# Moving GpSimd's elementwise work of a two-block network to VectorE and ScalarE

## The chip, the cores and the metric

The kernel runs on one core of a Trainium2 chip. The metric is the device time of one execution in microseconds (us). The engines are called as in the profile: PE (TensorE, the matmuls; PEld loads their weights), DVE (VectorE), ACT (ScalarE), POOL (GpSimd) and SP (SyncE, which issues DMAs).

## The reference

Everything is computed in fp32, for 256 tokens of width 1024. A first block has two layers (an mLSTM and a differential attention, each followed by a mixture of experts). A second block then runs two layers over two streams, the latent tokens `h` and 256 context tokens `hc`; each layer is a feed-forward, a mixer and a second feed-forward. Cut to what matters here:

```python
def pre(t, mm, i, gi):
    return rms_norm(t, g[gi]) * (1 + mm[:, :, i + 1]) + mm[:, :, i]
def post(t, y, mm, i, gi, wres):
    return t + wres * mm[:, :, i + 2] * rms_norm(y, g[gi])

h = post(h, swiglu(pre(h, m, 0, 0), ffn_wi[0], ffn_wo[0]), m, 0, 1, 0.5)     # hc alike
u, uc = pre(h, m, 3, 2), pre(hc, mc, 3, 2)
oc, kv_c = context_mix(uc @ w_in, qk_g, conv_w)      # last layer: only kv_c
o = latent_mix(u @ w_in, kv_c, cos, sin, qk_g, rpb, conv_w, rows)
h = post(h, o @ w_o, m, 3, 3, 1.0)                   # hc alike, but not in the last layer
h = post(h, swiglu(pre(h, m, 6, 4), ffn_wi[1], ffn_wo[1]), m, 6, 5, 0.5)
```

The mixers hold softmax attentions of 64-wide heads: six heads over latent and context keys (512), six with a position bias over a window of the latent keys and all context keys, and in the first layer twelve more of the context over its own 256 keys.

## The kernel before

Activations lie transposed: `xT` and `ctxT` hold the two streams as 8 slices of 128 features by 256 tokens. Each fp32 operand of a matmul is split into a high part that PE takes in one pass and the low rest, and a product is three matmuls (`mm3`, L381 to L383). Weights arrive by DMA as `raw` pieces; `chunks` makes the high part on ACT (L371) and the low part on DVE (L374). This goes on through the whole program.

The second block (`second_block`, from 1200 us on) runs six sublayers: feed-forward, mixer, feed-forward, twice. The first four carry both streams out, the last two only the latent one. Between two sublayers lies a transition, five in all. While a sublayer's output `y` comes out of PE, slice by slice and stream by stream, `Output.add` squares it (L497, L498 on ACT), takes its product with the old `x` (L499 on DVE), and adds these three 256-wide tiles into `acc` (L501, a 128x768 addition): on DVE for the last but one slice, else on POOL. After the last slice `sums` adds over the partitions with matmuls (L519), `rows` reads the sums (`rowsums`, L537), and `rstd` (L412 to L422) makes the reciprocal roots of `y` and of the new `x` with eleven tiny DVE instructions each; PE spreads a result over the partitions (L427). Then `update` goes slice by slice: `xs` is the scaled output (L561), `xT` takes it (L562, POOL but for the first slice), the new input is scaled (L569) and `split_sum` adds a shift and splits it into the parts `u` for the next matmuls: even slices with one ACT and one DVE instruction (L361, L362), odd ones with two on ACT and a subtraction on POOL (L357 to L359). `x_squares` (L461) does similar sums at the start of each block.

A mixer (`mix`) projects queries, keys and values, loads a position bias and turns its sign by 12 POOL subtractions (L904), and calls `attend` over units of two heads: six units of 512 keys in each of the two mixers, and six of 256 in the first. For a unit, `parts` splits keys and queries (high on ACT L838, low on POOL L839), PE makes scores, `softmax` takes the extreme on DVE (L818), exponentials with their sum on ACT (L822), the reciprocal on DVE (L824) and multiplies the row by it on POOL (L825). PE then transposes the weights (L860), an engine that the scheduler picks copies them out of PSUM (L861, ACT or DVE), and PE takes the values. While a unit's scores are made, the one before is transposed and multiplied; there are four buffers for `p`, two for `ysq`.

The order of every engine's instructions is not written by hand. A scheduler arranges the program from the written order, the dependences and its own estimate of each instruction, and chooses the engine of the free copies; so an instruction that moves to another engine shifts its neighbours too.

Of the kernel before, what the change touches and what calls it, by code (L numbers as in the profile page):

```python
# [13 lines left out]
AF = mybir.ActivationFunctionType  # L14
# [5 lines left out]
KT = 8  # L20
# [214 lines left out]
class Kernel:  # L235
# [114 lines left out]
        self.nc.scalar.activation(hi, src, AF.Copy)  # L350
        self.nc.vector.tensor_sub(lo, src, hi)  # L351

    def split_sum(self, hi, lo, src, col, by_pool=False):

        nc = self.nc
        if by_pool:
            nc.scalar.activation(src, src, AF.Identity, bias=col)  # L357
            nc.scalar.activation(hi, src, AF.Copy)
            nc.gpsimd.tensor_sub(lo, src, hi)  # L359
        else:  # L360
            nc.scalar.activation(hi, src, AF.Identity, bias=col)  # L361
            nc.vector.scalar_tensor_tensor(lo, src, col, hi, op0=ALU.add, op1=ALU.subtract)  # L362

    def chunks(self, ring, src, step=128):

# [86 lines left out]
    def x_squares(self, pool, s):  # L452

        nc = self.nc
        st = self.st()
        sums = []
        for k in range(KT):
            sq = pool.tile([128, S], F32, name="sq", **(dict(tag="sq", bufs=2) if k % 2 else dict(tag="xs", bufs=self.xs_bufs)))
            nc.scalar.activation(sq, self.xs(k, s), AF.Square)
            if k % 2:  # L460
                (nc.gpsimd if k < 4 else nc.vector).tensor_add(sums[-1], sums[-1], sq)  # L461
            else:
                sums.append(sq)
        for k, sq in enumerate(sums):
            for j in range(2):
                nc.tensor.matmul(st[:, j:j + 1], sq[:, j * 128:j * 128 + 128], self.ones[:, :1], start=(k == 0 and j == 0),
                                 stop=True, skip_group_check=True)
        return st[:, :2]
# [9 lines left out]
    class Output:  # L478
# [10 lines left out]
        def add(self, d, s):  # L489

            kern, nc = self.kern, self.kern.nc
            y = self.y(d, s)
            if d == 0:
                t = self.acc[s] = self.pool.tile([128, 3, S], F32, tag=f"acc{s}", name="acc", bufs=1)
            else:
                t = self.pool.tile([128, 3, S], F32, tag="pt", name="ysq", bufs=2)
            nc.scalar.activation(t[:, 0], y, AF.Square)  # L497
            nc.scalar.activation(t[:, 1], y, AF.Square, scale=self.gate(d, s))  # L498
            nc.vector.scalar_tensor_tensor(t[:, 2], y, self.gate(d, s), kern.xs(d, s), op0=ALU.mult, op1=ALU.mult)  # L499
            if 0 < d < KT - 1:  # L500
                (nc.vector if d == KT - 2 else nc.gpsimd).tensor_add(self.acc[s], self.acc[s], t)  # L501
            self.late.append(lambda: self.end(d, s, t))

        def go_on(self):
# [48 lines left out]
    def update(self, pool, u, s, out, gs, sh):  # L553

        nc = self.nc
        rb1, rb2 = out.rows(s)

        def add(k):
            if k < KT:
                t = pool.tile([128, S], F32, tag="xs", name="xs", bufs=self.xs_bufs)  # L560
                nc.vector.scalar_tensor_tensor(t, out.y(k, s), out.gate(k, s), rb1, op0=ALU.mult, op1=ALU.mult)  # L561
                (nc.gpsimd if k else nc.vector).tensor_add(self.xs(k, s), self.xs(k, s), t)  # L562

        for k in range(AHEAD):
            add(k)
        for k in range(KT):
            add(k + AHEAD)
            t = pool.tile([128, S], F32, tag="xs", name="xs", bufs=self.xs_bufs)
            nc.vector.scalar_tensor_tensor(t, self.xs(k, s), gs[:, k:k + 1], rb2, op0=ALU.mult, op1=ALU.mult)  # L569
            self.split_sum(u[:, k, 0], u[:, k, 1], t, sh[:, k:k + 1], k % 2)  # L570

    def scale_cols(self, pool, sc, g, ns, name):

# [240 lines left out]
    def softmax(self, pool, sc, n, scale=None):  # L814

        nc = self.nc
        mx = pool.tile([128, 4], F32, tag="mx", name="mx", bufs=8)
        nc.vector.tensor_reduce(mx[:, 0:1], sc[:, :n], axis=AX.X, op=ALU.min)  # L818
        if scale:
            nc.vector.tensor_mul(mx[:, 0:1], mx[:, 0:1], scale[0])  # L820
        p = pool.tile([128, 2 * S], F32, tag="p", name="p", bufs=4)
        nc.scalar.activation(p[:, :n], sc[:, :n], AF.Exp, bias=mx[:, 0:1], scale=scale[1] if scale else -1.0,  # L822
                             accum_out=mx[:, 1:2])
        nc.vector.reciprocal(mx[:, 2:3], mx[:, 1:2])  # L824
        nc.gpsimd.tensor_mul(p[:, :n], p[:, :n], mx[:, 2:3].to_broadcast([128, n]))  # L825
        return p

    def attend(self, ring, pool, units):
# [5 lines left out]
        def parts(q, k, nk, *_):  # L834

            out = ring.parts()
            for x, c in ((k[:, :nk], slice(0, nk)), (q, slice(512, 512 + S))):
                nc.scalar.activation(out[0][:, c], x, AF.Copy)  # L838
                nc.gpsimd.tensor_sub(out[1][:, c], x, out[0][:, c])  # L839
            return out  # L840

        def scores(qk, t, q, k, nk, v, vcols, out, bias, rs):
# [46 lines left out]
    def mix(self, ring, pool, l, u, out, u_home, proj_home):  # L889
# [11 lines left out]
        for t in range(2):  # L901
            nc.sync.dma_start(bias[:, t], A["rpb"][l, t])
            for h in range(6):
                nc.gpsimd.tensor_sub(bias[:, t, h], self.k("window_up"), bias[:, t, h])  # L904
        nc.vector.tensor_scalar(gq, self.v(f"qk_{l}_0"), -0.125, None, op0=ALU.mult)
        nq = TQ // 128
        offs = (0, 8, 8 + 2 * nq, 8 + 4 * nq)
# [957 lines left out]
```

## Time and profile before

| | us |
|---|---|
| runs | 2702.36, 2703.2, 2704.69 (median 2703.2) |
| the profiled execution | 2702.24 |
| its span | 2700.4 |
| busy: PE / PEld | 2476.7 (92%) / 1915.4 (71%) |
| busy: DVE / ACT / POOL | 1653.1 (61%) / 935.7 (35%) / 473.4 (18%) |

The span runs from the first to the last instruction of the profile. Busy shares are averages over stages with different limits; a row of idle time names what ended it.

### The profile page before, as it was taken

How to read it: one execution, taken by the hardware profiler on the slowest of the kernel's cores; microseconds unless marked ns; L12 is line 12 of the kernel's file. 1: busy time of each engine (PE TensorE's matmuls, PEld its weight loads, DVE VectorE, ACT ScalarE, POOL GpSimd, SP SyncE). 2: the span in 40 equal slices, each digit the busy share in tenths (PEclk: the TensorE clock that was granted, in tenths of full speed). 3: DMA queues.
4: the chain of work that ended last, by engine and by line, in shares of the span. 5: the costliest groups of instructions: out<-in, count | busy, mean ns of one | idle time of the engine just before them, and what ended most of it. 6: DMA issues, size and time to landing. Idle time of an engine off the chain costs nothing.

```text
span 2700.4 us, 38571 instructions
## 1 busy us (share of the span) xinstructions
PE 2476.7 (92%) x14614; PEld 1915.4 (71%) x14614; DVE 1653.1 (61%) x3421; ACT 935.7 (35%) x1641; POOL 473.4 (18%) x420
## 2 busy tenths in 40 slices
PE   3988997887999899999899999999899999898998
PEld 3874344566444688888775788888788888786997
DVE  7873125786222368656866777673858665958555
ACT  3541103564011232223327542222432223445543
POOL 2330101544000000002406420000400001534100
PEclk9989998888999899999899999999999999999999
DMA  8789997667999356532340236453247443322453
GB/s 320 276 327 410 420 419 261 232 211 298 381 398 419 141 185 221 168 120 88 135 138 1 79 110 209 154 190 91 74 148 226 155 150 97 118 83 94 160 178 123
DMA packets 123305, 540.62 MB, mean 200 GB/s; under 512 B 14688, under 2 KB 14944, under 8 KB 98272
## 3 DMA queue, kind: packets, MB, share of 16 engines
q1 hardware_dynamic: 123104, 538.00, 55.2%
q8 instruction: 119, 1.95, 0.3%
q14 instruction: 82, 0.67, 0.1%
HBM read 536.90 MB, written 1.05 MB: 199 GB/s over the span
## 4 chain that ended last, share of the span: by engine, by line
PE 56%; DVE 7%; issue 1%; ACT 1%; DMA 1%; POOL 0%; DVEq 0%; SPq 0%; ACTq 0%; POOLq 0%
PE mm L382 16%; PE mm L383 16%; PE mm L381 16%; DVE lo L374 2%; PE tp L383 1%; PE tp L382 1%; PE tp L381 1%; PE mm L868 1%; PE tp L860 1%; PE mm L848 1%; DVE ysq L499 1%; DMA raw<-in_w_ada_dram 1%; ACT hi L371 0%; DVE mx L818 0%; DVE rs_x L412 0%
## 5 line engine op out<-in xcount | busy, mean ns | idle before, releaser
L374 DVE TENSOR_TENSOR lo<-raw,hi 128x512 fp32r<-128x512 f32 (+1 forms) x780 | 574.7, 766 | 381.5 <-ACT hi L371 379.1
L371 ACT ACTIVATE hi<-raw 128x1024 fp32r<-128x1024 f32 (+1 forms) x390 | 404.7, 1044 | 872.3 <-PE mm L382 571.4
L381 PE MATMUL mm<-u,hi 128*128 128x512 f32 (+1 forms) x1608 | 572.8, 360 | 17.5 <-ACT hi L371 9.6
L383 PE MATMUL mm<-u,lo 128*128 128x512 f32 (+1 forms) x1608 | 576.8, 360 | 5.2 <-DVE lo L374 5.2
L382 PE MATMUL mm<-u,hi 128*128 128x512 f32 (+1 forms) x1608 | 578.2, 360 | 2.3 <-POOL u L359 1.3
L381 PEld LDWEIGHTS mm<-u,hi 128*128 128x128 f32 x1608 | 306.9, 193 | 64.5 <-ACT hi L371 11.2
L383 PEld LDWEIGHTS mm<-u,lo 128*128 128x128 f32 x1608 | 310.5, 193 | 49.1 <-DVE lo L374 6.9
L382 PEld LDWEIGHTS mm<-u,hi 128*128 128x128 f32 x1608 | 310.6, 193 | 47.3 <-DVE u L362 2.5
L382 PE MATMUL mm<-act,hi 128*128 128x512 f32 (+1 forms) x612 | 223.0, 364 | 0.1
L381 PE MATMUL mm<-act,hi 128*128 128x512 f32 (+1 forms) x612 | 222.3, 363 | 0.0
L383 PE MATMUL mm<-act,lo 128*128 128x512 f32 (+1 forms) x612 | 222.2, 363 | 0.0
L1691 PE MATMUL mm<-raw,xg 128*32 128x512 f32 x1696 | 199.2, 593 | 1.1 <-DMA raw<-in_moe_gu_dram 1.1
L623 DVE SCALAR_TENSOR_TENSOR junk<-raw,conds 128x1024 f32<-128x1024 f32 x128 | 155.6, 1222 | 66.3 <-DMA raw<-in_w_ada_dram 65.9
L620 POOL TENSOR_TENSOR raw<-raw,cond 128x1024 f32<-128x1024 f32 x48 | 119.9, 2502 | 244.7 <-DMA raw<-in_w_ada_dram 224.8
L501 POOL TENSOR_TENSOR acc<-acc,ysq 128x768 f32<-128x768 f32 x45 | 92.5, 2065 | 394.0 <-DVE ysq L499 348.8
L623 DVE SCALAR_TENSOR_TENSOR raw<-raw,conds 128x1024 f32<-128x1024 f32 x128 | 156.6, 1229 | 2.4
L628 POOL TENSOR_TENSOR mod<-mod,vecs 128x16 f32<-128x16 f32 (+1 forms) x28 | 10.3, 366 | 764.7 <-DVE raw L623 721.4
L1691 PEld LDWEIGHTS mm<-raw,xg 128*32 128x32 f32 x1696 | 63.0, 110 | 112.3 <-issue 107.6
L381 PEld LDWEIGHTS mm<-act,hi 128*128 128x128 f32 x612 | 117.5, 192 | 18.7 <-issue 1.2
L382 PEld LDWEIGHTS mm<-act,hi 128*128 128x128 f32 x612 | 117.7, 192 | 18.2 <-DVE act L351 0.7
L383 PEld LDWEIGHTS mm<-act,lo 128*128 128x128 f32 x612 | 117.5, 192 | 17.2
L1723 DVE TENSOR_TENSOR hy<-hy,tp 128x512 f32<-128x512 f32 x56 | 38.2, 686 | 149.3 <-PE tp L1720 149.1
(458 smaller groups left out, 4102.5 us busy)
## 6 DMA issues: line engine op xcount, KB each, us to landing
raw<-in_moe_gu_dram SPq DMA_DIRECT2D x122, 1024.0 KB, 17.8
raw<-in_w_ada_dram SPq DMA_DIRECT2D x200, 512.0 KB, 4.5
raw<-in_ffn_wi_dram SPq DMA_DIRECT2D x176, 512.0 KB, 4.3
raw<-in_moe_down_dram SPq DMA_DIRECT2D x63, 1024.0 KB, 17.8
raw<-in_ffn_wo_dram SPq DMA_DIRECT2D x48, 448.0 KB, 3.9
raw<-in_w_k_dram SPq DMA_DIRECT2D x32, 512.0 KB, 3.9
raw<-in_ffn_wo_dram SPq DMA_DIRECT2D x24, 512.0 KB, 4.2
raw<-in_ffn_wo_last_dram SPq DMA_DIRECT2D x22, 512.0 KB, 4.1
```

The costliest lines, as they stand in the source:

```text
L371: self.mark = self.nc.scalar.activation(hi[:, :m], raw[:, c:c + m], AF.Copy)
L374: self.nc.vector.tensor_sub(lo[:, i:e], raw[:, c + i:c + e], hi[:, i:e])
L381: nc.tensor.matmul(out, lh, rh, start=start, stop=False, skip_group_check=mixed)
L382: nc.tensor.matmul(out, lh, rl, start=False, stop=False, skip_group_check=mixed)
L383: nc.tensor.matmul(out, ll, rh, start=False, stop=stop, skip_group_check=mixed)
L499: nc.vector.scalar_tensor_tensor(t[:, 2], y, self.gate(d, s), kern.xs(d, s), op0=ALU.mult, op1=ALU.mult)
L501: (nc.vector if d == KT - 2 else nc.gpsimd).tensor_add(self.acc[s], self.acc[s], t)
L620: nc.gpsimd.tensor_mul(out, rows, c)
L623: nc.vector.scalar_tensor_tensor(out, rows, 1.0, c, op0=ALU.mult, op1=ALU.mult, accum_out=mod[:, t, s:s + 1])
L848: nc.tensor.matmul(sc[:, :nk], qk[a][half, 512 + t * 128:640 + t * 128], qk[b][half, :nk], start=(i == 0), stop=(i == 2))
L1691: nc.tensor.matmul(ps[t:t + 32], x[:, t:t + 32], w[i][:, s], start=first, stop=last)
L1723: nc.vector.tensor_add(yv, yv, tp)
```

## The change

Five kinds of POOL instructions go elsewhere. The additions of squares (L501), the low parts of queries and keys (L839), the turning of the bias (L904) and the additions of `x_squares` (L461, in both blocks) are issued to DVE. The odd slices of `split_sum` are made like the even ones, on ACT and DVE. The softmax's multiplication by the reciprocal (L825) becomes an ACT activation whose scale is that reciprocal. In `update` L562 stays on POOL. The function `split_sum` is five lines shorter, so that after it a line of the changed kernel has a number five lower (L501 is L496, L825 is L820).

```diff
@@ -350,16 +350,11 @@
         self.nc.scalar.activation(hi, src, AF.Copy)
         self.nc.vector.tensor_sub(lo, src, hi)
 
-    def split_sum(self, hi, lo, src, col, by_pool=False):
-
-        nc = self.nc
-        if by_pool:
-            nc.scalar.activation(src, src, AF.Identity, bias=col)
-            nc.scalar.activation(hi, src, AF.Copy)
-            nc.gpsimd.tensor_sub(lo, src, hi)
-        else:
-            nc.scalar.activation(hi, src, AF.Identity, bias=col)
-            nc.vector.scalar_tensor_tensor(lo, src, col, hi, op0=ALU.add, op1=ALU.subtract)
+    def split_sum(self, hi, lo, src, col):
+
+        nc = self.nc
+        nc.scalar.activation(hi, src, AF.Identity, bias=col)
+        nc.vector.scalar_tensor_tensor(lo, src, col, hi, op0=ALU.add, op1=ALU.subtract)
 
     def chunks(self, ring, src, step=128):
 
@@ -458,7 +453,7 @@
             sq = pool.tile([128, S], F32, name="sq", **(dict(tag="sq", bufs=2) if k % 2 else dict(tag="xs", bufs=self.xs_bufs)))
             nc.scalar.activation(sq, self.xs(k, s), AF.Square)
             if k % 2:
-                (nc.gpsimd if k < 4 else nc.vector).tensor_add(sums[-1], sums[-1], sq)
+                nc.vector.tensor_add(sums[-1], sums[-1], sq)
             else:
                 sums.append(sq)
         for k, sq in enumerate(sums):
@@ -498,7 +493,7 @@
             nc.scalar.activation(t[:, 1], y, AF.Square, scale=self.gate(d, s))
             nc.vector.scalar_tensor_tensor(t[:, 2], y, self.gate(d, s), kern.xs(d, s), op0=ALU.mult, op1=ALU.mult)
             if 0 < d < KT - 1:
-                (nc.vector if d == KT - 2 else nc.gpsimd).tensor_add(self.acc[s], self.acc[s], t)
+                nc.vector.tensor_add(self.acc[s], self.acc[s], t)
             self.late.append(lambda: self.end(d, s, t))
 
         def go_on(self):
@@ -567,7 +562,7 @@
             add(k + AHEAD)
             t = pool.tile([128, S], F32, tag="xs", name="xs", bufs=self.xs_bufs)
             nc.vector.scalar_tensor_tensor(t, self.xs(k, s), gs[:, k:k + 1], rb2, op0=ALU.mult, op1=ALU.mult)
-            self.split_sum(u[:, k, 0], u[:, k, 1], t, sh[:, k:k + 1], k % 2)
+            self.split_sum(u[:, k, 0], u[:, k, 1], t, sh[:, k:k + 1])
 
     def scale_cols(self, pool, sc, g, ns, name):
 
@@ -822,7 +817,7 @@
         nc.scalar.activation(p[:, :n], sc[:, :n], AF.Exp, bias=mx[:, 0:1], scale=scale[1] if scale else -1.0,
                              accum_out=mx[:, 1:2])
         nc.vector.reciprocal(mx[:, 2:3], mx[:, 1:2])
-        nc.gpsimd.tensor_mul(p[:, :n], p[:, :n], mx[:, 2:3].to_broadcast([128, n]))
+        nc.scalar.activation(p[:, :n], p[:, :n], AF.Copy, scale=mx[:, 2:3])
         return p
 
     def attend(self, ring, pool, units):
@@ -836,7 +831,7 @@
             out = ring.parts()
             for x, c in ((k[:, :nk], slice(0, nk)), (q, slice(512, 512 + S))):
                 nc.scalar.activation(out[0][:, c], x, AF.Copy)
-                nc.gpsimd.tensor_sub(out[1][:, c], x, out[0][:, c])
+                nc.vector.tensor_sub(out[1][:, c], x, out[0][:, c])
             return out
 
         def scores(qk, t, q, k, nk, v, vcols, out, bias, rs):
@@ -901,7 +896,7 @@
         for t in range(2):
             nc.sync.dma_start(bias[:, t], A["rpb"][l, t])
             for h in range(6):
-                nc.gpsimd.tensor_sub(bias[:, t, h], self.k("window_up"), bias[:, t, h])
+                nc.vector.tensor_sub(bias[:, t, h], self.k("window_up"), bias[:, t, h])
         nc.vector.tensor_scalar(gq, self.v(f"qk_{l}_0"), -0.125, None, op0=ALU.mult)
         nq = TQ // 128
         offs = (0, 8, 8 + 2 * nq, 8 + 4 * nq)
```

Of the 72 copies L861 (then L856), ACT had 47 and DVE 25; ACT has 20 and DVE 52 after it.

DVE, in the first transition, from the last weights' low part to `rstd`; `rowsums` reads the latent stream's sums. Before:

```order
L374 TENSOR_TENSOR lo<-raw,hi 128x512
L537 COPY rowsums<-st 96x256
L374 TENSOR_TENSOR lo<-raw,hi 128x512
L541 COPY sums<-tp 128x6
L412 TENSOR_SCALAR rs_x<-sums 128x2
L413 TENSOR_SCALAR rs_y<-rs_x 128x2
L414 TENSOR_SCALAR rs_z<-rs_x 128x2
L417 TENSOR_SCALAR rs_h<-rs_x 128x2
L415 TENSOR_TENSOR rs_t<-rs_y 128x2
L416 TENSOR_TENSOR rs_t<-rs_t,rs_z 128x2
L418 SCALAR_TENSOR_TENSOR rs_t<-rs_t 128x2
L419 SCALAR_TENSOR_TENSOR rs_y<-rs_t,rs_y 128x2
```

After:

```order
L369 TENSOR_TENSOR lo<-raw,hi 128x512
L532 COPY rowsums<-st 96x256
L496 TENSOR_TENSOR acc<-acc,ysq 128x768
L536 COPY sums<-tp 128x6
L369 TENSOR_TENSOR lo<-raw,hi 128x512
L407 TENSOR_SCALAR rs_x<-sums 128x2
L710 TENSOR_TENSOR yT<-yT,mm 128x256
L408 TENSOR_SCALAR rs_y<-rs_x 128x2
L409 TENSOR_SCALAR rs_z<-rs_x 128x2
L412 TENSOR_SCALAR rs_h<-rs_x 128x2
L410 TENSOR_TENSOR rs_t<-rs_y 128x2
L494 SCALAR_TENSOR_TENSOR ysq<-yT,gate,ctxT 128x256
```

An addition of `acc` (L496), which POOL made before, now stands between reading the sums and `rstd`, and one L710 (then L715) inside `rstd`.

ACT, at the start of the first mixer's attention; `p` are the softmax's rows, `nr` is the scale of the exponentials, `pt` the transposed weights. Before:

```order
L822 ACTIVATE p,mx<-mm,mx,nr 128x512 x6
L838 ACTIVATE hi<-proj 128x512
L838 ACTIVATE hi<-proj 128x256
L861 COPY pt<-tp 128x4x128
L822 ACTIVATE p,mx<-mm,mx,nr 128x512 x2
L838 ACTIVATE hi<-proj 128x512
L838 ACTIVATE hi<-proj 128x256
L350 ACTIVATE o<-mm 128x256
L822 ACTIVATE p,mx<-mm,mx,nr 128x512 x2
```

After:

```order
L817 ACTIVATE p,mx<-mm,mx,nr 128x512 x2
L820 ACTIVATE p<-p,mx 128x512 x2
L817 ACTIVATE p,mx<-mm,mx,nr 128x512 x2
L820 ACTIVATE p<-p,mx 128x512 x2
L817 ACTIVATE p,mx<-mm,mx,nr 128x512 x2
L820 ACTIVATE p<-p,mx 128x512 x2
L817 ACTIVATE p,mx<-mm,mx,nr 128x512 x2
L820 ACTIVATE p<-p,mx 128x512 x2
L350 ACTIVATE o<-mm 128x256
```

The exponentials (L822, now L817) alternate in pairs with the multiplications by the reciprocal (L820), of which each needs DVE's reciprocal of its exponential; six exponentials stood in a row before.

## Rows read from the trace of the kernel before

**Rows 1.** the page's chain that ended last, shares of the span by engine

```profile
PE 56%; DVE 7%; issue 1%; ACT 1%; DMA 1%; POOL 0%; DVEq 0%; SPq 0%; ACTq 0%; POOLq 0%
```

**Rows 2.** busy time of each engine, one stretch: PE, PEld, DVE, ACT, POOL, PEclk, DMA, GB/s

```profile
2475.00:2500.00 25.00, 13.39 (x88) 10.09 (x87) 21.97 (x55) 7.63 (x15) 6.36 (x6) 0.69 0.35 114
```

**Rows 3.** PE's timeline in four transitions: start, us, line, idle before and releaser

```profile
1283.59 0.28 PE L383 MATMUL mm<-act,lo 128*128 128x256 f32 x1
...
1283.71 0.28 PE L381 MATMUL mm<-act,hi 128*128 128x256 f32 x1
...
1286.96 0.66 PE L427 MATMUL tp<-consts,rs_y 128*128 128x128 f32 x2 [2.98 <-DVE rs_y L422]
...
1552.80 1.02 PE L519 MATMUL st<-acc,consts 128*32 128x256 f32 x6 [3.23 <-DVE acc L501]
...
1928.01 0.40 PE L427 MATMUL tp<-consts,rs_y 128*128 128x128 f32 x2 [2.98 <-DVE rs_y L422]
...
2487.00 1.07 PE L519 MATMUL st<-acc,consts 128*32 128x256 f32 x6 [4.26 <-DVE acc L501]
```

**Rows 4.** stretches of the attentions, columns as in rows 2

```profile
1443.10:1449.63 6.53, 6.53 (x45) 3.90 (x45) 4.70 (x12) 5.60 (x14) 6.53 (x9) 1.00 0.01 3
...
1463.38:1469.75 6.37, 6.09 (x46) 3.92 (x44) 5.27 (x15) 5.48 (x15) 5.39 (x7) 1.00 0.00 0
...
2418.00:2458.00 40.00, 38.51 (x240) 24.39 (x240) 32.93 (x79) 30.84 (x71) 28.84 (x28) 0.93 0.15 43
```

**Rows 5.** POOL's groups from 1200 us: count, busy, mean ns, idle before and releasers

```profile
L501 POOL TENSOR_TENSOR acc<-acc,ysq 128x768 f32<-128x768 f32 x45 | 92.5, 2065 | 394.0 <-DVE ysq L499 348.8 <-DVE lo L374 28.8 <-ACT ysq L498 16.4
...
L825 POOL TENSOR_TENSOR p<-p,mx 128x512 f32<-128x512 f32 x48 | 51.3, 1085 | 21.8 <-DVE mx L824 15.6 <-DVE mx L820 5.3 <-PE mm L848 0.8
...
L839 POOL TENSOR_TENSOR lo<-proj,hi 128x512 fp32r<-128x512 f32 x12 | 15.5, 1290 | 79.3 <-ACT hi L838 79.3
...
L904 POOL TENSOR_TENSOR bias<-consts,bias 128x256 f32<-128x256 f32 x24 | 19.4, 847 | 2.3 <-DMA bias<-in_rpb_dram 2.3
```

**Rows 6.** DVE's groups of the same stretch, columns as in rows 5

```profile
L499 DVE SCALAR_TENSOR_TENSOR ysq<-yT,gate,xT 128x256 f32<-128x256 f32 x35 | 31.5, 903 | 4.0 <-ACT yT L989 2.2
...
L499 DVE SCALAR_TENSOR_TENSOR ysq<-yT,gate,ctxT 128x256 f32<-128x256 f32 x28 | 13.4, 478 | 0.1
...
L501 DVE TENSOR_TENSOR acc<-acc,ysq 128x768 f32<-128x768 f32 x9 | 8.6, 953 | 0.5
```

**Rows 7.** DVE's timeline in the first transition, columns as in rows 3

```profile
1264.14 0.69 DVE L715 TENSOR_TENSOR yT<-yT,mm 128x512 f32<-128x512 f32 x1
...
1279.88 0.41 DVE L537 COPY rowsums<-st 96x256 f32<-96x256 f32 x1
...
1281.00 1.62 DVE L412 TENSOR_SCALAR rs_x<-sums 128x2 f32<-128x2 f32 x1
...
1295.74 0.48 DVE L569 SCALAR_TENSOR_TENSOR xs<-xT,gs,tp 128x256 f32<-128x256 f32 x1
```

**Rows 8.** DVE's timeline at the end of the second mixer

```profile
2480.11 0.41 DVE L989 COPY yT<-mm 128x256 f32<-128x256 f32 x1
...
2481.03 2.92 DVE L374 TENSOR_TENSOR lo<-raw,hi 128x512 fp32r<-128x512 f32 x2
...
2483.88 0.41 DVE L989 COPY yT<-mm 128x256 f32<-128x256 f32 x1
```

**Rows 9.** ACT's groups from 1200 us, columns as in rows 5

```profile
L498 ACT ACTIVATE ysq<-yT,gate 128x256 f32<-128x256 f32 x63 | 31.1, 494 | 0.0
...
L822 ACT ACTIVATE p<-mm,mx,nr 128x512 f32<-128x512 f32 x24 | 18.5, 775 | 6.2 <-POOL p L825 2.4 <-PE tp L860 1.8 <-DVE mx L820 1.7
...
L838 ACT ACTIVATE hi<-proj 128x256 fp32r<-128x256 f32 x24 | 9.9, 418 | 0.0
...
L838 ACT ACTIVATE hi<-proj 128x512 fp32r<-128x512 f32 x12 | 7.5, 628 | 29.7 <-issue 29.7
```

**Rows 10.** DVE's timeline at the first mixer's projections

```profile
1329.96 1.14 DVE L374 TENSOR_TENSOR lo<-raw,hi 128x512 fp32r<-128x512 f32 x1 [6.13 <-ACT hi L371]
```

## The prediction

> **What bounds the kernel now.** I read the 40 slices of the page first, then the table by stretches of 25 us, then the chain of waits, then PE's and DVE's timelines where PE is not full. The chain is PE for 56% and DVE for 7% of the span, and POOL for 0% [rows 1]: no work of POOL is on it by name. Through the feed-forward layers PE is full, and nothing that POOL does there counts. The time that is to be won or lost lies in two kinds of places. The first are the five transitions of the second block, where one sublayer's output is closed (squares, sums, rstd) and the next one's input is made. In the last of them PE works for 13.39 of 25 us at a granted clock of 0.69, while DVE works for 21.97 [rows 2]. The long holes of PE are 2.98 us at 1286.96, 3.23 at 1552.80, 2.98 at 1928.01, one like it in the transition at 2310, and 4.26 at 2487.00; DVE releases each of them [rows 3]. The second kind are the attentions, where a unit of two heads takes 6.4 to 7.0 us and PE, ACT, DVE and POOL are all close to full; POOL is busy for 6.53 of 6.53 us in the unit at 1443.10 [rows 4]. So I look at what the change does to DVE's list in the first kind and to ACT's in the second.
>
> **Additions of squares (L501, 45 of them, ten in each of four transitions and five in the last).** On POOL one takes 2065 ns [rows 5]; the nine that DVE has already take 953 ns each [rows 6], so DVE takes on 45 x 0.95 = 43 us at most, and 39 by the 0.87 us from one start to the next that I take. Against it stands what the additions on POOL cost DVE now. The same product L499 takes 903 ns for the first stream, which often meets an addition on POOL, and 478 for the second, which rarely does [rows 6]. L412, two numbers in each partition, takes 1.62 us at 1281.00 while POOL adds; its like take some 0.16. L715 at 1264.14, which has one input in PSUM, takes its usual 0.69 in the middle of an addition [rows 7]. Summed over all DVE instructions that lie under an L501 of POOL and are longer than the first quartile of their shape, the excess is 60.9 us, or 1.35 for each addition. So DVE gives up 61 and takes on 39: about 22 us less on DVE, and not a load.
>
> The Trainium skill, "SBUF — State Buffer", section "Who interferes with whom", states that VectorE and GpSimd share one pair of ports as an exclusive lock, held for a whole instruction, and that VectorE meets GpSimd's reads there when both its inputs lie in SBUF. The trace agrees for L499, held (903 ns), and for L715, not held (0.69 us). By that rule the stalls end with the additions on POOL, which speaks for -14.1 below; were they due to something else that stays, DVE would be 39 us heavier and rival 3 would be the case to expect.
>
> What of it is on the path? In the first transition DVE runs without a pause from the rowsums at 1279.88 to the first product of the next input at 1295.74, 15.86 us [rows 7], and PE waits for what stands in that list. Adding up the after list by starts one after the other (0.60 us for a 512-wide low part, 0.87 for an addition, 0.40 for a product, 0.34 for L715, 0.07 to 0.19 for the small ones) gives 14.4 us, since two stalls of about 1.5 go and two additions come. The list also begins 0.9 to 1.7 us earlier, because DVE is no longer late for the last columns: that is -2.5 to -3.2. I take -3.0. The transitions at 1928 and 2310 have the same rows, -3.0 each. The one at 1552 has fewer stalls in the list: -1.6. In the last one a column takes DVE 3.77 us (2480.11 to 2483.88), with a pair of low parts stretched to 2.92 by POOL [rows 8]; PE's 24 matmuls of a column start 0.12 us apart where nothing holds them, as at 1283.59 and 1283.71 [rows 3], which is 2.9. DVE's after list for a column (copy 0.34, low parts 1.2, product 0.40, addition 0.87) adds to 2.8: the hole of 4.26 shrinks to the 0.7 that an addition's end needs, -3.5. **Sum of the transitions: -14.1; by bounds -18 (every long hole of PE to under 0.5) to -4 (the additions that now stand in DVE's list ahead of rstd take the places of the stalls, and only the last transition gains).**
>
> **The softmax's division (L825).** POOL needs 1085 ns for 512 columns, 48 times [rows 5], and does 24 of 256 columns. ACT has no such row. The nearest are L838 at 512 columns, 628 ns, and at 256, 418, without a pointer, and L498 at 256 with a pointer, 494 [rows 9]; starts lie about 0.1 closer than these. So 628 + 76 - 100 gives 0.60 us at 512, and 494 - 100 gives 0.39 at 256. (Bounds: 0.51 if the pointer costs nothing, 0.71 if nothing overlaps.) In a unit of 512 ACT is busy for 5.60 us at 1443.10 and 5.48 at 1463.38 [rows 4], over half of it four exponentials of 775 ns [rows 9]. Add 4 x 0.60 = 2.4 and take off some 0.8, one or two of the L861 copies that the new order gives to DVE (ACT has 20 of 72, before 47), and 7.2 us are left. PE has 6.09 of work in the unit at 1463.38 [rows 4]. ACT becomes the engine that sets the pace: 7.2 to 7.5 for 6.7 now. For six units in the first mixer and six in the second (40 us from 2418, [rows 4], 6.67 each) that is +4.5 and +5.0. The six units of 256 need 4 x 0.39 = 1.6 more of ACT in about 5.4 us, of which some 0.9 was free: +1.5.
>
> The Trainium skill, "ScalarE: Activation LUTs", section "Rules for kernel authors", speaks against this move: it wants multiplications on VectorE, up to about 3 times faster there, in bf16 and with one source. Here, in fp32, the rows show no such difference at 256 columns: 494 ns on ACT [rows 9], 478 on DVE [rows 6]. By the rule a division on DVE would have cost 0.2 us, and the 0.4 us of difference, 48 times, would be 19 us of ACT's time that another engine could have had cheaper: it would make the +11 below avoidable, not smaller.
>
> **Sum of the attentions: +11; by bounds -3 (PE stays the pace, and POOL's share of its waits goes) to +18.**
>
> **Low parts and bias, with one answer each.** L839 (12 of 1290 ns on POOL [rows 5] and 24 of 256 columns) costs DVE about 12 x 0.61 + 24 x 0.34 = 15 us over the 18 units, 0.9 in each, hidden behind ACT's 7.2: DVE is busy for some 5 us of a unit and takes 0.9 and the L861 copies on, so 6.5 to 6.9. If that cover is gone it is part of the +18. L359 on the odd columns gives way to the even ones' form (L361, L362), in lists beside PE's stream; ACT sheds one instruction for each: 0, from -1 to +1. L904 (12 per mixer of 847 ns [rows 5]) costs DVE 12 x 0.35 = 4.2 us, in the pause of 6.13 us that it has before 1329.96 [rows 10], but copies of the first heads' products stand behind some of them: +0.5, from 0 to +3. L461's additions lie where PE is full: 0.
>
> **Sum.** -14.1 + 11 + 0.5 = -2.6. The profiled execution took 2702.24 us with a span of 2700.4; this gives 2699.6, and the median of the runs, 2703.2, is 1.0 above the profiled one: 2700.6. I say 2700.
>
> **Rivals.**
> 1. The attention stays PE's or gets better: the division leaves the slow engine, POOL's 6.53 of 6.53 us in a unit is the true pace, and ACT, never held, hides 2.4 us more in pauses it has (6.53 less 5.60, 0.93 in that unit). For it speaks that POOL is named in PE's waits at the first units; against it, that ACT's sum is above PE's. -14 - 1 to -3: **2686 to 2689**.
> 2. The other side: ACT becomes a queue in which order hurts. A division waits for DVE's reciprocal, and behind it stand the next pair's exponentials and the L861 copies for which PE's transposes wait. Each unit then takes 7.7 to 7.9. From 0.9 us more per unit on (18 units, +16 to +20) it outweighs the transitions: 2703.2 - 14 + 20 = **2709**, up to 2712. For it: DVE copies and low parts are queued ahead of reciprocals. Against it: exponentials come in pairs, so the second covers the first's reciprocal.
> 3. The transitions gain only the last one's 4 us, since additions replace stalls, and the attentions lose 11: **2710**.
> 4. The change reaches no path in either place, the holes being latency: **2703**.
>
> **How the numbers follow.** Forecast 0.42 (its own range 2694 to 2706), rival 1 0.26, rival 2 0.16, rival 3 0.08, rival 4 0.08. A measurement of this kernel can tell about 0.2%, 5.4 us, from no change: faster is below 2697.8, slower above 2708.6. The forecast gives 0.14 faster, 0.24 same, 0.04 slower; rival 1 0.26 faster; rivals 2 and 3 0.16 slower and 0.08 same; rival 4 same, 0.08. So 0.40, 0.40 and 0.20. The range takes in rival 1's 2687 and most of rival 2: 2687 to 2711.
>
> **What would show it.** POOL without L501 and L825. L499's two streams alike at about 0.48, L412 and L422 at 0.16. PE's holes of 3 us in the transitions shrunk to 1 or less, and the one at 2487 to under 1. In the attentions ACT above 90% and a unit of 7.2 to 7.5. What would make the prediction wrong: a unit at 6.5 (rival 1) or near 8 (rival 2), or holes of PE that end at an addition of DVE instead of at rstd (rival 3).

## The result: 18 us slower

The changed kernel takes 2721.8 us (median of 4 runs, 2721.4 to 2724.0) beside 2703.9 us for the kernel before in the same session: a ratio of 1.0066, 95% interval 1.0048 to 1.0083. The forecast was 2700 with a range of 2687 to 2711. Its profiled execution has a span of 2719.9 us.

The profile page of the changed kernel, the chain that ended last (to be read beside [rows 1]; line numbers after 350 are five lower than before):

```profile
PE 60%; DVE 4%; ACT 2%; issue 1%; DVEq 0%; ACTq 0%
```

DVE's share of the chain has fallen from 7% to 4%, PE's has risen from 56% to 60% and ACT's from 1% to 2%. The kernel's groups from 1200 us on, ACT and then DVE (line, engine, operation, tiles, count, busy, mean ns, idle before and releaser; to be read beside [rows 5, 6, 9]):

```profile
L820 ACT ACTIVATE p<-p,mx 128x512 f32<-128x512 f32 x48 | 33.1, 722 | 6.3 <-DVE mx L819 6.0
L820 ACT ACTIVATE p<-p,mx 128x256 f32<-128x256 f32 x24 | 11.6, 503 | 1.3 <-DVE mx L819 1.1
...
L496 DVE TENSOR_TENSOR acc<-acc,ysq 128x768 f32<-128x768 f32 x54 | 50.4, 952 | 2.7 <-ACT ysq L493 2.0
L357 DVE SCALAR_TENSOR_TENSOR u<-xs,mod,u 128x256 fp32r<-128x256 f32 x72 | 43.6, 613 | 0.8 <-ACT u L356 0.7
...
L494 DVE SCALAR_TENSOR_TENSOR ysq<-yT,gate,xT 128x256 f32<-128x256 f32 x35 | 16.8, 481 | 2.7 <-ACT yT L984 2.3
L494 DVE SCALAR_TENSOR_TENSOR ysq<-yT,gate,ctxT 128x256 f32<-128x256 f32 x28 | 13.4, 479 | 0.1
```

The product L494 (L499 before) takes 481 and 479 ns for the two streams, where it took 903 and 478: the stall is gone. The multiplication L820 costs ACT 722 ns at 512 columns and 44.7 us in all.

To see where the time went I set the two traces side by side at instructions that both have (the last projection of a mixer, the first output copy, a fixed step of each feed-forward) and took the shift from one to the next, from 1250 us on. The part before that is left out (2.6 us of the 19.5 by which the two spans differ): the instructions there come up to 18 us apart in the profiled executions, and e3 and e7 below, which leave the first block's order as it was, differ by 13 us there. In us against before:

| | four two-stream transitions | first mixer's attention | second mixer's attention | last transition | sum |
|---|---|---|---|---|---|
| forecast | -10.1 | +6.0 | +5.0 | -3.5 | -2.6 |
| the change | -2.9 | +18.1 | +6.7 | -4.9 | +16.9 |

3 us of the first column belong to before's profiled execution alone: at 1356 DVE waits 2.80 us there for weights of other work that fills gaps,

```profile
1356.14 1.23 DVE L623 SCALAR_TENSOR_TENSOR junk<-raw,conds 128x1024 f32<-128x1024 f32 x1 [2.80 <-DMA raw<-in_w_ada_dram]
```

which e2 and e5, equal to before in that stretch, do not show (they stand 3.4 and 3.3 us lower). Against these the four transitions together gain nothing at all.

**The attentions.** The two mixers' attentions, the first mixer's in each kernel (columns as in [rows 4]: us, PE, PEld, DVE, ACT and POOL busy, PEclk, DMA share, GB/s). Before:

```profile
1426.30:1507.20 80.90, 75.97 (x457) 47.60 (x454) 58.05 (x171) 60.67 (x166) 54.25 (x66) 0.94 0.09 27
```

After, the whole of it and four pieces of 2 us:

```profile
1428.50:1527.50 99.00, 91.14 (x457) 53.49 (x454) 69.01 (x209) 77.44 (x194) 0.00 (x0) 0.88 0.07 22
...
1444.00:1446.00 2.00, 2.00 (x12) 1.05 (x11) 0.00 (x0) 0.18 (x1) 0.00 (x0) 0.50 0.00 0
1450.00:1452.00 2.00, 1.80 (x9) 1.11 (x8) 1.88 (x8) 2.00 (x7) 0.00 (x0) 1.00 0.03 8
1452.00:1454.00 2.00, 0.98 (x4) 0.46 (x3) 2.00 (x6) 2.00 (x6) 0.00 (x0) 0.90 0.00 0
...
1460.00:1462.00 2.00, 2.00 (x11) 1.06 (x8) 0.14 (x1) 0.10 (x1) 0.00 (x0) 0.50 0.00 0
```

ACT is busy for 77.4 of 99.0 us, 78%. The forecast had it full, above 90%; it is not, and yet the stretch is 18 us longer. The pieces show how. At 1450 to 1454 ACT works all the time, PE waits for an exponential (L817), and is down to 0.98 of 2 us. At 1444 and at 1460 it is the other way round: PE works all the time, at a granted clock of 0.50 (1.2 GHz), with ACT and DVE nearly idle. The two work by turns, and PE's clock falls after its pauses: one of 2.27 us ends at 1432.69 and the granted clock is 0.50 from 1433.1 on, one of 1.02 us ends at 1453.49 and it is 0.50 again from 1453.6 on. With the two levels 1 and 0.50, (1 - PEclk) x 2 is the share of a piece at the lower one; summed over pieces of 2 us, the first mixer's attention holds 23.9 us at the lower level, and 10.2 before.

The loss is not spread evenly. The first value matmul (L863, before L868) of each of the first six units starts at 1441.6, 1456.2, 1468.7, 1476.6, 1484.1 and 1490.2, and before at 1440.2, 1446.6, 1453.6, 1460.4, 1467.4 and 1474.0. The first two steps take 27.1 us for 13.4, which is 13.7 of the 18.1 us, and 15.4 of those 27.1 us are at 1.2 GHz; the next two, 7.9 and 7.5, are close to the forecast of 7.2 to 7.5. The second mixer has no more time at 1.2 GHz than before (6.8 us in both) and loses 6.7 for a forecast of 5.0.

**The transitions.** PE's holes in the first transition and the one at the end of the second mixer (to be read beside [rows 3]):

```profile
1290.98 0.63 PE L514 MATMUL st<-acc,consts 128*32 128x256 f32 x6 [2.44 <-DVE acc L496]
...
1294.62 0.66 PE L422 MATMUL tp<-consts,rs_y 128*128 128x128 f32 x2 [1.71 <-DVE rs_y L417]
...
1316.35 0.66 PE L422 MATMUL tp<-consts,rs_y 128*128 128x128 f32 x2 [3.52 <-DVE rs_y L417]
...
2506.20 0.63 PE L514 MATMUL st<-acc,consts 128*32 128x256 f32 x6 [0.75 <-DVE acc L496]
```

and DVE's list in the first transition (to be read beside [rows 7]):

```profile
1280.89 0.41 DVE L532 COPY rowsums<-st 96x256 f32<-96x256 f32 x1
...
1295.32 0.48 DVE L564 SCALAR_TENSOR_TENSOR xs<-xT,gs,tp 128x256 f32<-128x256 f32 x1 [0.84 <-PE tp L422]
```

The hole of 4.26 us has become 0.75, as forecast. The list from the rowsums to the first product of the next input is 14.43 us long for 15.86 (forecast 14.4), and it starts 1.6 us earlier against the shift of 2.6 at 1250, so the first stream's input comes 3.0 us earlier (forecast 3.0). What takes that away again is the second stream: its rstd reaches PE after a hole of 3.52 us at 1316.35. Before, the hole in that place was 1.93 us:

```profile
1314.41 0.66 PE L427 MATMUL tp<-consts,rs_y 128*128 128x128 f32 x2 [1.93 <-DVE rs_y L422]
```

### The profile page after: what moved, and what is told of

It reads as the page before. It is cut to its first block, busy times and chain, and to the rows that moved or that the text cites. A ratio compares the mean times of both kernels' runs of the same rounds, so it can differ in the third digit from the quotient of the medians.

```text
span 2719.9 us, 38348 instructions
## 1 busy us (share of the span) xinstructions
PE 2488.0 (91%) x14614; PEld 1916.4 (70%) x14614; DVE 1668.0 (61%) x3597; ACT 947.3 (35%) x1650; POOL 229.8 (8%) x199
## 3 DMA queue, kind: packets, MB, share of 16 engines
q8 instruction: 118, 1.93, 0.3%
## 4 chain that ended last, share of the span: by engine, by line
PE 60%; DVE 4%; ACT 2%; issue 1%; DVEq 0%; ACTq 0%
PE mm L376 17%; PE mm L377 16%; PE mm L378 16%; PE mm L863 2%; PE tp L378 1%; PE tp L377 1%; PE tp L376 1%; PE mm L843 1%; PE tp L855 1%; DVE lo L369 1%; PE mm L929 1%; PE mm L930 1%; ACT p L817 1%; PE mm L928 1%; ACT p L820 0%
## 5 line engine op out<-in xcount | busy, mean ns | idle before, releaser
L369 DVE TENSOR_TENSOR lo<-raw,hi 128x512 fp32r<-128x512 f32 (+1 forms) x780 | 532.2, 709 | 377.2 <-ACT hi L366 375.4
L1686 PE MATMUL mm<-raw,at 128*32 128x512 f32 x880 | 110.0, 595 | 10.7 <-ACT at L1701 8.1
L1696 DVE TENSOR_TENSOR xn<-xn,mm 128x512 f32<-128x512 f32 x14 | 9.6, 688 | 172.7 <-PE mm L1686 160.0
## 6 DMA issues: line engine op xcount, KB each, us to landing
raw<-in_moe_gu_dram SPq DMA_DIRECT2D x122, 1024.0 KB, 18.1
raw<-in_moe_down_dram SPq DMA_DIRECT2D x63, 1024.0 KB, 18.1
```

The lines of the kernel that those rows point to most:

```text
L369: self.nc.vector.tensor_sub(lo[:, i:e], raw[:, c + i:c + e], hi[:, i:e])
L1686: nc.tensor.matmul(ps[t:t + 32], x[:, t:t + 32], w[i][:, s], start=first, stop=last)
```

## The experiments

Ratios are to the kernel before, run on the same chip in the same session. "A" is the shift of the two attentions together, "T" that of all five transitions, by the same instructions as above (profiled execution, us). Every T holds the 3.3 us of before's own: e2, whose transitions are those of before, stands at -4.8, so that a T of -3.7 to -4.8 is no gain.

**e1 to e4: the parts apart.** e1 puts L820 of the changed kernel back on POOL, e4 puts it on DVE; e2 and e3 are the kernel before with one part each.

```diff
 e1, e4 (in the changed kernel)
-        nc.scalar.activation(p[:, :n], p[:, :n], AF.Copy, scale=mx[:, 2:3])
+        nc.gpsimd.tensor_mul(p[:, :n], p[:, :n], mx[:, 2:3].to_broadcast([128, n]))         # e1
+        nc.vector.tensor_scalar(p[:, :n], p[:, :n], mx[:, 2:3], None, op0=ALU.mult)         # e4
 e2: in the kernel before, the line above with nc.scalar.activation
 e3: in the kernel before
-                (nc.vector if d == KT - 2 else nc.gpsimd).tensor_add(self.acc[s], self.acc[s], t)
+                nc.vector.tensor_add(self.acc[s], self.acc[s], t)
```

> The changed kernel with one part undone: the softmax's multiplication by the reciprocal (L825 of before) is back on POOL. Theory A, the attentions lose 18 us in the first mixer and 7 in the second because this multiplication stands in ACT's list: the attentions come back to before, about 2697 us (2721.8 - 24.8), first mixer's attention about 72 us long, no second stretch of half clock in it. Rival B, the low parts of queries and keys on DVE (L839) or the new order of all engines bring the loss: 2715 or more, second stretch of half clock still there.

> The kernel before with one part of the change alone: the softmax's multiplication (L825) on ACT. Theory A: about 2703 + 22 to 25 = 2725 to 2728, slower than the whole change, whose transitions gained some 8 us. Rival B: 2701 to 2706.

> The kernel before with one part alone: all additions of squares (L501) on DVE. Theory A with the transitions as the two traces show them (0 to -3 in each of the first four, -5 in the last): 2694 to 2697. The prediction's own sum for this part, -14: 2689. If the additions gain only in the last transition: 2698.

> The changed kernel with the softmax's multiplication on DVE, as a product with a scalar of each partition. ACT's list is as in e1, and so is the order of PE in the attentions. If DVE needs 0.6 us for 512 columns, as for a subtraction, a unit of 512 takes it some 8.3 us for 6.5 now and the attentions lose 15 to 20: about 2715. If it needs about half of that, DVE stays under PE's time and the result is that of e1, about 2697.

| | ratio, 95% interval | A | T |
|---|---|---|---|
| e1 division on POOL | 1.0005, 0.9991 to 1.0019 | +4.3 | -4.5 |
| e2 division on ACT alone | 1.0103, 1.0078 to 1.0127 | +31.4 | -4.8 |
| e3 squares on DVE alone | 0.9960, 0.9943 to 0.9978 | +0.1 | -15.1 |
| e4 division on DVE | 1.0075, 1.0056 to 1.0094 | +23.3 | -3.7 |

e2 alone costs 28 us (0.0103 x 2701), and e1, without it, is level with before, with 10.2 us at 1.2 GHz in the first mixer as before (its attention is 83.4 us long for 80.9 by the ends used here; the 72 us of the expectation ran from the first exponential to the last): the multiplication on ACT alone brings the loss of the attentions and more, +31.4 for the change's +24.7, and rival B of these runs falls. The parts don't add up, since the +4.3 of e1 would come on top; e2 holds 37.5 us at 1.2 GHz in the first mixer, the change 23.9, and why it has more stays open. Not as expected was e1's total. It should have kept the transitions' gain, and the gain isn't there, though e3 has it in full. e4 shows the second surprise: its instruction is short,

```profile
L820 DVE TENSOR_SCALAR p<-p,mx 128x512 f32<-128x512 f32 x48 | 22.7, 478 | 0.0
```

478 ns for 1085 on POOL, and the kernel is still 20 us slower. The engine isn't all that differs here. The expectation took PE's order and ACT's list to be those of e1, but the scheduler gave PE another order in e4, and ACT 63 of the 72 copies (48 in e1), and with these the first mixer holds 27.3 us at 1.2 GHz. No run holds PE's order with the multiplication on DVE, so how much of e4's loss is the order's is open. In these runs a slow POOL with little else to do is a better place than either of two faster engines that are not full.

**e5 and e6: PE's order held.** The scheduler's order differs between before and after, so the loss could be the order's. Both kernels again, with PE's instructions in `attend` held in the written order:

```diff
-                    nc.tensor.matmul(sc[:, :nk], ...)
+                    self.tc.keep_in_program_order(nc.tensor.matmul(sc[:, :nk], ...))
 the transposes (L860) and the value matmuls (L868) alike
```

> The kernel before, with PE's instructions of the attentions held in the order in which they are written: six score matmuls, eight transposes, six scores, eight transposes, eight value pairs. It is the base for e6, whose engines differ and whose PE order is the same. Both theories: within 3 us of before, about 2701 to 2706, since before's own order is nearly this one.

> The changed kernel with the same held order of PE in the attentions. Theory order (the attentions lose because the scheduler, given other durations, lumps PE's scores, transposes and values otherwise, so that PE and ACT work by turns): the attentions are back near those of e5, about 2696 to 2701 in all. Theory time (the multiplication in ACT's list delays the exponentials and through them PE, whatever PE's order): 2714 to 2722 as the change itself.

e5: 1.0005 (0.9987 to 1.0023), A +3.2. e6: 1.0070 (1.0052 to 1.0089), A +20.6. With one order of PE most of the loss stays, 17.4 us of A from e5 to e6, and 0.0065 in the ratios, so PE's order isn't its main cause: theory time holds. The profiled executions leave 4 us to the order if e6 is set beside the change (20.6 for 24.7), and 7 if e5 is its base; the ratios cannot tell these. The loss has another shape, though: the long first two units of the change are not there, and the first six units start 7.1 to 10.2 us apart, for 6.4 to 7.7 in e5.

**e9 to e12: what the multiplication costs.** All four are e6 with one edit; e9 and e10 leave out the softmax's division:

```diff
-        nc.scalar.activation(p[:, :n], p[:, :n], AF.Copy, scale=mx[:, 2:3])
+        nc.scalar.activation(p[:, :n], p[:, :n], AF.Copy, scale=self.ones[:, :1])     # e9; e10: line left out
-            nc.any.tensor_copy(pt[:, :nk // 128, ...], ...)
+            nc.vector.tensor_copy(pt[:, :nk // 128, ...], ...)                        # e11
 e12: the score matmul with i == 0 made twice (start=True, stop=True, then again with start=True)
```

> e6 (the change, PE's order in the attentions held) with the softmax's rows multiplied on ACT by a column of ones instead of the reciprocal: the same instruction in ACT's list, but it no longer waits for DVE. Left out: the softmax's division. Theory length (what costs is the time that 72 more instructions take in ACT's list, between the exponentials and the copies for which PE waits): within 3 us of e6, ratio 1.006 to 1.008. Theory wait (a multiplication at the head of ACT's list waits for DVE's reciprocal and holds up the rest): near e5, 0.998 to 1.002.

> e6 without the multiplication at all. Left out: the softmax's division. Both theories: the attentions at or below those of e5, the transitions 5 to 8 us shorter than before: ratio 0.995 to 0.998. If it stays above 1.002, something else in the change costs in the attentions (low parts on DVE).

> e6 with all 72 copies of transposed weights (L861) on DVE. In e6 most of PE's waits in the attentions end with such a copy on ACT. Theory length, in the form that these copies stand behind the multiplications in ACT's list: the attentions shorten by 6 to 15 us, ratio 1.001 to 1.005. If DVE, which then has some 6 us of work in a unit of 512, is as late as ACT: 1.006 or more.

> e6 with the first matmul of each scores tile made twice (the second overwrites it): 72 more matmuls, some 14 us of PE at full clock, and nothing else. Theory clock (of the 13 us that the first mixer's attention loses in e6 against e5 about 7 are stretches of half clock, and these come since PE pauses at ACT): PE pauses less, the half-clock stretches of the attentions shrink, and the time rises by less than 7 us or falls, 1.004 to 1.009. If the clock has no part in it, the work adds up where PE isn't waiting: 1.010 to 1.013.

| | ratio, 95% interval | A | first mixer's attention at 1.2 GHz, us |
|---|---|---|---|
| e6 | 1.0070, 1.0052 to 1.0089 | +20.6 | 20.5 |
| e9 no wait for the reciprocal | 1.0049, 1.0026 to 1.0072 | +21.6 | 17.1 |
| e10 no multiplication | 0.9966, 0.9950 to 0.9983 | -0.1 | 6.8 |
| e11 all copies on DVE | 1.0087, 1.0056 to 1.0118 | +28.8 | 17.1 |
| e12 more work for PE | 1.0053, 1.0028 to 1.0078 | +20.5 | 10.2 |

The first mixer's attention in e6, in e9, in e10 and in e12, in this order (columns as above):

```profile
1430.20:1524.20 94.00, 76.02 (x455) 47.19 (x453) 64.82 (x201) 79.62 (x203) 0.00 (x0) 0.89 0.07 23
```

```profile
1419.10:1513.20 94.10, 74.34 (x458) 46.24 (x455) 67.16 (x203) 78.51 (x200) 0.00 (x0) 0.91 0.08 23
```

```profile
1425.80:1506.20 80.40, 67.45 (x457) 44.28 (x454) 58.40 (x185) 62.49 (x171) 0.00 (x0) 0.96 0.09 27
```

```profile
1428.40:1519.80 91.40, 75.98 (x505) 48.72 (x502) 63.56 (x197) 80.69 (x207) 0.00 (x0) 0.94 0.08 24
```

e9's stretch is as long as e6's, 94.1 and 94.0 us: the wait for the reciprocal has no part in it there. The whole kernel's intervals of e6 and e9 overlap and would leave room for a small one. e10 takes the multiplication away and the stretch is 80.4 us, 13.7 less than in e9. So it is the length of the multiplication, and not its wait, that costs. The 24 multiplications of 512 columns and 24 of 256 in this stretch take 29.4 us of ACT (722 and 503 ns each), but e10 relieves ACT by only 16 us (78.5 to 62.5) and DVE by 8.8 (67.2 to 58.4), since the scheduler gives ACT 57 of the 72 copies there and 27 in e9. So about half of the multiplications' length is a length of the end, though ACT idles for 15.6 of 94.1 us in e9. The same step on POOL, 1085 ns long at 512 columns, costs hardly anything there: e5's stretch, with it and the low parts on POOL, is 81.4 us. What fits all of these is that PE, ACT and DVE hand each other the same few tiles, each serving its list in order, so that time put into a list in which others' work waits lengthens the round. That is argued; no run changed the number of buffers or the order of ACT's list.

e11 came out against its expectation, a gain of 6 to 15 us from copies that no longer stand behind the multiplications in ACT's list. In the two mixers it takes 13.7 us of work off ACT and puts 15.6 on DVE, and A grows by another 8 (2.4 us in the first mixer, 5.8 in the second); the ratios of e11 and e6 overlap. So ACT is not the only list in which time costs.

e12 gives PE 72 more matmuls, some 14 us at full clock by their distance of 0.23 us at 512 columns and 0.12 at 256 (an estimate), and loses nothing that can be measured against e6. In the first mixer the stretch even becomes shorter, 91.4 for 94.0, with the time at 1.2 GHz halved; in the second it becomes 2.5 us longer, with 13.6 us at 1.2 GHz for 10.2. Where the extra work kept the clock up it paid for itself, which supports that the clock is part of the loss in the first mixer. How large a part stays open: e9 has less of the lower level than e6 and the same length. In the change itself the 15.4 us at 1.2 GHz in the first two units would be 7.7 at full clock, if PE was the engine waited for all through them (an estimate).

**e7, e8, e13 and e14: where the transitions' gain went.** e7 is e3 with the odd slices of `split_sum` as in the change. e8 is e3 with L839, L904 and L461 on DVE, `split_sum` and the division as before. e13 and e14 are these two with L562 on DVE:

```diff
-                (nc.gpsimd if k else nc.vector).tensor_add(self.xs(k, s), self.xs(k, s), t)
+                nc.vector.tensor_add(self.xs(k, s), self.xs(k, s), t)
```

> The kernel before with two parts alone: additions of squares on DVE (e3) and the odd slices of split_sum made by ACT and DVE. Theory: the changed kernel loses some 7 of the 15 us that e3 gains in the transitions because DVE's L362 now comes twice as often and lies under POOL's L562: second-stream holes of PE of 3 us instead of 1.7, and the time 6 to 8 us above e3, at a ratio of 0.998 to 1.000. Rival (the bias and the low parts are what costs): ratio as e3, 0.995 to 0.997.

> The kernel before with the additions of squares, the low parts of queries and keys, the bias and the additions of x_squares on DVE; split_sum and the softmax's multiplication as before. By the theory of e7 this keeps most of e3's gain: ratio 0.996 to 0.998 (low parts and bias cost 1 to 4 us). By its rival it is like e1, 1.000.

> e7 (additions of squares and the odd slices' low parts on DVE) with the additions to the residual streams (L562) on DVE too, so that nothing of POOL runs in the transitions. e7 stands at 0.9994, e3, without the split, at 0.996. Theory lock (the split costs because L362 lies under POOL's L562, 0.84 us for 0.47): L362 is 0.47 throughout and the time falls to 0.996 to 0.998. Theory list (it costs because DVE has four more instructions in each update ahead of the second stream's rstd): the seven additions of 0.34 us in each update lengthen the list by 2.4 us, the lock gives 1.6 back, and the time stays or rises: 0.999 to 1.003.

> e8, the fastest so far (0.9948), with the additions to the residual streams (L562) on DVE. Theory list: each update is 2 us longer for DVE, four of them stand before a second stream: 0.996 to 0.999. Theory lock: POOL's L562 costs DVE 7.9 us in e8, and without it the time falls to 0.993 to 0.995.

| | ratio, 95% interval | A | T | second stream's hole at about 1950 |
|---|---|---|---|---|
| before | 1 | 0 | 0 | 1.09 |
| e3 | 0.9960, 0.9943 to 0.9978 | +0.1 | -15.1 | 1.09 |
| e7 | 0.9994, 0.9976 to 1.0012 | +0.4 | -6.4 | 3.02 |
| e13 | 0.9982, 0.9963 to 1.0001 | +0.4 | -7.1 | 3.85 |
| e8 | 0.9948, 0.9923 to 0.9973 | +3.6 | -17.2 | 1.09 |
| e14 | 0.9984, 0.9966 to 1.0001 | +5.7 | -5.9 | 3.02 |

The odd slices cost 9 us (e7 against e3), and with the low parts, bias and x_squares alone the gain stays (e8, whose ratio came out below the 0.996 to 0.998 that was expected). The group of L362 and the second stream's rstd at PE, in e7 and in e13:

```profile
L362 DVE SCALAR_TENSOR_TENSOR u<-xs,mod,u 128x256 fp32r<-128x256 f32 x72 | 43.0, 604 | 0.8 <-ACT u L361 0.7
...
1947.45 0.47 PE L427 MATMUL tp<-consts,rs_y 128*128 128x128 f32 x2 [3.02 <-DVE rs_y L422]
```

```profile
L362 DVE SCALAR_TENSOR_TENSOR u<-xs,mod,u 128x256 fp32r<-128x256 f32 x72 | 33.9, 480 | 1.4 <-ACT u L361 1.4
...
1949.01 0.66 PE L427 MATMUL tp<-consts,rs_y 128*128 128x128 f32 x2 [3.85 <-DVE rs_y L422]
```

Without POOL in the transitions L362 takes 480 ns for 604, so the stall under L562 is real, and taking it away helps little if at all (T -7.1 for -6.4), since the additions that come to DVE make its list longer. e14 tells which of the two counts: it has no odd slices on DVE, only the additions, and loses 11 us of T against e8, with the hole of 3.02 that e7 has. It is the list (for the odd slices by that same hole; no run has them alone without L562 on POOL): while DVE works through the first stream's update, the second stream's rstd stands behind it, and whatever is put into that update moves PE's second hole. e14's ratio lies where theory list had it, e13's a little below; theory lock is refuted by e14.

**e8** is the version that beats both: 2687.6 us (2683.0 to 2689.5) beside 2701.9, a ratio of 0.9948. It is the change without the division on ACT and without the odd slices.

## Why the prediction was wrong, step by step

- **Additions of squares: right in the mechanism, and close in size.** The term was -14.1. Less the 3.3 us that e5 shows to be the own of before's profiled execution, e3, which moves this part alone, gains 15.1 - 3.3 = 11.8 in the five transitions (10.8 by its ratio), and e8 17.2 - 3.3 = 13.9. The stall was the cause: DVE's list came out at 14.43 us for 14.4, the last hole at 0.75 for 0.7. The signs that were named came only in part. PE's holes of 3 us did not shrink to 1 or less: in the first transition they are 2.44 and 1.71, and the first of them ends at an addition on DVE, which was to be rival 3's sign. But e3 has the same holes there, 2.43 and 1.59, and gains all the same, and only 3.7 of e8's us lie in the last transition. So rival 3's mechanism falls, though in the change itself the first four transitions gain nothing, as it said; what eats their gain is the next term.
- **"L359 on the odd columns gives way to the even ones' form ...: 0, from -1 to +1": wrong.** It measures +9 (e7 against e3). The step looked for cover in the wrong place: beside PE's stream the low parts are hidden, but DVE's update of the first stream stands in front of the second stream's rstd, and 4 more instructions of 0.4 us go before it (in e7 27 of the 72 L362 are stretched to some 0.8 us, in e3 10 of 36). PE's hole at the second stream grows by 1.8 to 2.2 us in each of the first three transitions (3.51 for 1.72, 2.81 for 0.66, 3.02 for 1.09). The sum was made over PE's holes ahead of the first stream and took the update as neutral.
- **"Sum of the attentions: +11": wrong, by a wrong mechanism.** Measured +24.7. The step compared ACT's sum for a unit (7.2 us) with PE's (6.09 to 6.7) and let the larger set the pace. Its parts were near: 722 ns of busy time at 512 columns, for 0.60 from start to start, and ACT is indeed busy for 17 us more in the first mixer. But no engine was full: ACT was busy for 78%. Most of the miss lies in the first mixer, +18.1 for +6.0, and there in the first two units, where PE and ACT work by turns and PE runs at 1.2 GHz for 15.4 of 27.1 us. The time of a unit is not the maximum of the engines' sums, and the bound of +18 was made with that maximum; the clock had no term. What each of the two, the longer round and the clock, makes of the miss stays open. (By its rows the bounds of one multiplication are 0.53 and 0.70, not 0.51 and 0.71, which changes nothing.)
- **Rival 2** had the side and, with 2709 to 2712, the nearest time. A multiplication in ACT's list that delays what stands behind it is near to what the runs show, but by its length: the wait for the reciprocal, which the rival named, has no part in it in e9. e6 speaks only of PE's order, and the order of ACT's list was not tested. Its chance of 0.16 was too low.
- **Low parts, bias: nearly right.** A is -0.1 in e10, where they are on DVE and nothing multiplies, and +4.3 and +3.6 in e1 and e8, where POOL still multiplies: hidden as said, but for up to 4 us there.
- **The rule of the Trainium skill** in "ScalarE: Activation LUTs", section "Rules for kernel authors", that multiplications go to VectorE, agrees with the instruction's own time here: 478 ns on DVE, 722 on ACT, in fp32. It doesn't agree with the kernel's: e4 is no faster than the change (1.0075 and 1.0066). What was said behind it, that VectorE's division would make the loss avoidable, is not borne out: e4 loses 23.3 us in the attentions.
- **The lock** of the Trainium skill, "SBUF — State Buffer", section "Who interferes with whom": the trace agrees again, L494 at 481 ns without L501 on POOL, L362 at 480 without L562 and 604 with it. e13 and e14 add that ending a stall was worth nothing that could be measured where the work that made it came into the same list.

## What to carry to other kernels

Where engines hand tiles round in a loop, do not count a step that moves between engines only against its new engine's free time: here some half of its length became a length of the end on an engine that was busy for 83%. An engine that is slow but has little else to do can be the best place. Moving work off a neighbour that stalls you pays where the stall stands ahead of what PE waits for, and costs where the moved work itself stands there: list, for each moved instruction, what is queued behind it for the next consumer. And test the parts of such a change apart: here one gained 11 us, and two others lost 28 and 9.

## What the runs showed of the hardware

The tiny L412, two numbers in each partition with a single input in SBUF, was held for 1.62 us while POOL added ([rows 7]) and takes 0.16 in the changed kernel, so that the size of an instruction was no protection. A multiplication of 512 columns by a scalar of each partition takes 478 ns on DVE, less than a subtraction of two tiles of that size (688 ns for the low parts of the changed kernel). And some 14 us of added matmuls cost nothing that could be measured in e12, where PE had pauses; in the first mixer the time at 1.2 GHz halved with them.
